# A hybrid encoder layer: zero products at the start, a DMA order, and three re-orderings around TensorE

## The chip, the cores and the metric

One core of a Trainium2 chip runs the whole layer in one launch. The metric is the device time of one execution in microseconds (us), as the median of several runs. TensorE (PE in the profile) multiplies and transposes, VectorE (DVE) and GpSimd (POOL) do elementwise work, ScalarE (ACT) evaluates functions and copies, SyncE (SP) issues most of the DMA transfers. PEld is TensorE's loading of weights.

## The reference

All in float32, one batch, 1024 tokens of width 1024. Three residual sub-layers:

```python
h = rms_norm(x, mix_pre_g)
proj = h @ w_in                        # u (512) | q, k, v (512 each) | 8 forget logits
y_ssm = s5_mixer(u, ...)               # diagonal state-space model, then GLU:
#   g = gelu(y);  out = g * sigmoid(g @ glu_w + glu_b)
y_fox = forgetting_attention(q, k, v, f_logit)        # 8 heads of 64, causal
y_mix = concat([rms_norm(y_ssm, ssm_out_g), rms_norm(y_fox, fox_out_g)])
x = x + rms_norm(y_mix @ w_out, mix_post_g)

h = rms_norm(x, xa_pre_g)              # cross-attention, 4 heads, 256 memory tokens
x = x + rms_norm(memory_cross_attention(h, rms_norm(mem, mem_g), ...), xa_post_g)

h = rms_norm(x, ffn_pre_g)             # SwiGLU, hidden width 2816
x = x + rms_norm((silu(h @ w_gate) * (h @ w_up)) @ w_down, ffn_post_g)
```

## The kernel before, in words

**Precision and products.** Each float32 operand is split into a rounded high part and a low part (`split`: a copy on ACT at L113 and a subtraction on DVE at L115 or L117). A product is then three matmuls, high by high, high by low and low by high (`mm3`, L122 to L124), accumulated in PSUM.

**Front (L896 to L926).** x comes transposed, in eight tiles of 128 rows by 1024 tokens; the u columns of `w_in` come as eight tiles of 128 by 512 (`u_load`). For each k one x tile and one weight tile are loaded and split, and `u_part` adds 24 matmuls into eight banks, four of pool `g` (`psg`) and two double ones of pool `s`. The first x tile is loaded and split in two halves (`x_fetch(xts, 0, 2)`, `x_split(..., 2)`), both ahead of the first weight tile in SP's queue.

**Projections and the state-space branch (L868 to L890).** The q, k and v projections run on TensorE while DVE computes the state-space scan. q and k go to DRAM (`qk_d`) and come back a head at a time. `ssm_out` (L629) then makes the branch's output: two slabs (`s_`), four groups of banks each (`b`), every group evacuated by a gelu on ACT (L639); then transposes and splits (L647, L649). The v tiles' evacuation is L310.

**Fox, GLU and fillers (L961 to L1002).** `fox` walks through 64 units, eight heads by eight blocks of 128 queries: `scores` (matmuls L733 and L734, DVE sum and minimum L740, exponential L742, normalisation L747), two units later `turn` (transposes L764, copied out of PSUM at L767 on DVE or L769 on ACT in turns), then `values` (L778). `prepare` loads the next head's q and k (L711, L712) and copies and splits them (L715, L716, L718); `behind()` orders those ACT copies after the last exponential that was issued, and before the first exponential there is nothing to order them after. Between fox units, `paced` steps the generator `fillers`: the rest of v, the GLU (`glu`: 12 matmuls, tanh L673, L674, L675, split, square L680, running sum L681 in `acc`, for four channel tiles by two token halves), the sums over channels for each token (`token_sums`, sixteen narrow matmuls L237, copied out at L238), `glu_stats` (the reciprocal root `r_s`), the memory's load, and `out_ssm`: row products of 12 matmuls into one bank of `g`, evacuated with the scale `r_s` on ACT (L836) and stored by SP (L839).

**The rest.** Output projection and first residual (L1018 to L1040), cross-attention, then the FFN with its products in a seven-multiplication scheme (L1260, L1518). At the end `take` and `quarter` process each quarter of the output: a DVE sum (L1462), its square on ACT with the row sum (L1453), the multiplication by the gain on POOL (L1459), and `finish`: `rsqrt_mean` (L137 to L145), the residual (L1497) and the store.

**Order.** A planner orders each engine's instructions ahead of time, by program order, priorities (`tc.high_priority`) and its own estimate of when each is ready; on the chip every engine then runs its list strictly in that order. `tc.issue_after(ins)` puts the instructions of a block that run on the engine of `ins` behind it in that list; it adds no wait. PSUM: four banks in pool `g`, used by nearly every product and transpose, and two double banks in pool `s`.

Of the kernel before, what the change touches and what calls it, by code (L numbers as in the profile page):

```python
# [9 lines left out]
F32 = mybir.dt.float32  # L10
# [7 lines left out]
P = 128  # L18
# [22 lines left out]
EVB = 13  # L41
OPB = 10


# [8 lines left out]
def layer(ctx: ExitStack, tc: tile.TileContext, a, out):  # L53
# [575 lines left out]
    def ssm_out():  # L629
        U, T, SS, mo = ssm_made  # L630
        for s_ in range(2):
            go = slab([P, 2, L, P], F32)
            with tc.high_priority(offset=boost):
                for b in range(4):
                    ps = g_ps([P, 4, NC])
                    for g in range(4):
                        pe.matmul(ps[:, g], U[s_][:, 4 * b + g], T[s_][:, 4 * b + g], start=True, stop=False)
                        pe.matmul(ps[:, g], SS[s_][:, 4 * b + g], mo[s_][:, 4 * b + g], start=False, stop=True)
                    act.activation(out=go[:, b // 2].rearrange("c j (g i) -> c g j i", i=16)[:, 4 * (b % 2):4 * (b % 2) + 4],  # L639
                                   in_=ps.rearrange("c g (j i) -> c g j i", i=16), func=AF.Gelu_apprx_tanh)  # L640
            yield
# [11 lines left out]
    def glu(ys):  # L653
# [9 lines left out]
        for ct in range(4):  # L663
            cs = slice(ct * P, (ct + 1) * P)
            hl = slab([P, 2, S])
            for h in range(2):
# [17 lines left out]
                yield  # L684
        token_sums(sv, acc)
        ys_stat.append(sv)

    def glu_stats():
        sv, = ys_stat
        tables("natural_log_exp_and_others")  # L690
        rsqrt_mean(r_s, sv, 512, 4 * EPS)


    def fox(yf):
# [3 lines left out]
        def prepare(h):  # L698
# [7 lines left out]
            for hf in range(2):  # L706
# [7 lines left out]
                with behind():  # L714
# [3 lines left out]
                    split(ka[:, 0, hs], ka[:, 1, hs], kd, lo_eng=eng)  # L718

        last = []  # L720

# [28 lines left out]
        def turn(h, t):  # L750
# [9 lines left out]
            for k0 in range(0, t + 1, 4):  # L760
# [4 lines left out]
                o = pt[:, k0:k0 + n, odd * P:(odd + 1) * P]  # L765
                if (t + k0 // 4) % 2:
                    dve.tensor_copy(o, tp[:, :n])  # L767
                else:
                    act.activation(out=o, in_=tp[:, :n], func=AF.Copy)  # L769
# [56 lines left out]
    def out_ssm(ys):  # L826
        for cc in range(4):
            wh, wl = load_w(a["w_out_s"][cc], 256)
            for j0 in range(0, NT, 2):
                o = t2t([P, 2, 256])  # L830
                for j in range(j0, j0 + 2):
                    ts = slice(j * P, (j + 1) * P)
                    ps = g_ps([P, 256])
                    for k in range(4):
                        mm3(ps, ys[k][:, 0, ts], ys[k][:, 1, ts], wh[:, k], wl[:, k], k == 0, k == 3)
                    act.activation(out=o[:, j - j0], in_=ps, func=AF.Copy, scale=r_s[:, j:j + 1])  # L836
                    if j == j0:
                        yield
# [16 lines left out]

    ys, yf, gl, ys_stat, r_mem, gate, ssm_made = [], [], [], [], [], [], []

# [38 lines left out]
    with tc.high_priority(offset=boost):  # L896
        xts = []
        x_fetch(xts, 0, 2)
        xs = [[slab([P, 2, S]) for _ in range(KT // 2)] for _ in range(2)]
        xH, xL = ([x[k // 2][:, k % 2] for k in range(KT)] for x in xs)  # L900
        acc_x = tt("d")
        banks = [g_ps([P, 512]) for _ in range(4)]
        banks += [b[:, h * 512:h * 512 + 512] for b in (s_ps([P, S]) for _ in range(2)) for h in range(2)]
        ws = [u_load(0)]
        x_split(xts, (xH, xL), 0, 2)
        u_part(banks, 0, ws[0], xH[0], xL[0])
# [55 lines left out]
    def fillers():  # L962
# [3 lines left out]
        rows = out_ssm(ys)  # L966
        glu_stats()
        for _ in mem_load(r_mem[0], mem):
# [479 lines left out]

    LO, HI = slice(0, 512), slice(512, 1024)

    def square(t, j, h, src):
# [3 lines left out]
    def quarter(t, j, hs):  # L1455

        c = acc[t][j][:, hs]
        square(t, j, 0 if hs is LO else 1, c)
        pool.tensor_tensor(out=c, in0=c, in1=g_fq[:, hs], op=ALU.mult)  # L1459

# [27 lines left out]
    def finish(t, j):  # L1488
# [7 lines left out]
        for hs in (LO, HI):  # L1496
            dve.scalar_tensor_tensor(out=x2[:, hs], in0=acc[t][j][:, hs], scalar=r, in1=x2[:, hs],  # L1497
                                     op0=ALU.mult, op1=ALU.add)
            if last:
# [90 lines left out]
```

## Time and profile before

| | us |
|---|---|
| median of 3 runs (lowest to highest) | 1423.64 (1420.83 to 1426.41) |
| the profiled execution | 1424.64 |
| its span, first to last instruction | 1422.9 |
| PE busy in the span | 1380.0 |
| DVE, ACT, POOL busy | 956.9, 653.7, 406.0 |
| mean granted TensorE clock | 0.989 of full |

A row of the trace gives the start and the duration in us, engine, line, operation and tiles, and in square brackets the idle time of the engine ahead of it with what ended it. A row of waits gives the waiting engine, tile and line, what it waited for, then the total in us, how often, and the longest.

### The profile page before, as it was taken

The numbers are of one execution on the slowest core, as the hardware profiler recorded it, in microseconds if no ns is written. First come the engines' busy times: TensorE is split into PE (matmuls) and PEld (weight loads), VectorE is DVE, ScalarE is ACT, GpSimd is POOL, SyncE is SP. The second block draws the span as 40 slices with busy tenths as digits, with TensorE's granted clock in tenths as the row PEclk, the third lists the DMA queues.
The fourth block names the chain that finished last, engine by engine and source line by source line (L and its number), as shares of the span: only waits on it lengthen the run. The fifth ranks groups of instructions, "written<-read, shape, count | busy, mean of one in ns | idle before, by whom it ended". The sixth has DMA issues, their size and how long they took to land.

```text
span 1422.9 us, 20364 instructions
## 1 busy us (share of the span) xinstructions
PE 1380.0 (97%) x7342; PEld 1165.1 (82%) x7342; DVE 956.9 (67%) x1703; ACT 653.7 (46%) x1293; POOL 406.0 (29%) x428
## 2 busy tenths in 40 slices
PE   7999989899999898999999999999999999999997
PEld 6889889789888686788888788888888888888886
DVE  8839945956566676645457677787777676565565
ACT  6372336666676555533434533333333334544351
POOL 0001000013333134002021367687666661000021
PEclk9999999999999998999999999999999999999999
DMA  6324653155643758324537355554444446965544
GB/s 208 95 77 134 172 177 105 58 166 178 202 146 106 183 184 249 116 74 135 176 115 258 123 185 185 179 172 164 151 156 155 170 148 228 346 210 192 178 163 163
DMA packets 110230, 234.22 MB, mean 165 GB/s; under 512 B 11816, under 2 KB 46632, under 8 KB 110000
## 3 DMA queue, kind: packets, MB, share of 16 engines
q1 hardware_dynamic: 94496, 179.91, 39.8%
q0 software_dynamic: 15632, 53.00, 10.4%
q8 instruction: 58, 0.95, 0.3%
q14 instruction: 44, 0.36, 0.1%
HBM read 166.81 MB, written 74.71 MB: 170 GB/s over the span
## 4 chain that ended last, share of the span: by engine, by line
PE 59%; DVE 1%; ACT 0%; issue 0%; DVEq 0%; ACTq 0%
PE x L1260 17%; PE g L1260 13%; PE x L1518 7%; PE g L1518 7%; PE x L123 2%; PE x L124 2%; PE x L122 2%; PE g L122 2%; PE g L123 2%; PE g L124 2%; PE g L1048 1%; PE g L1156 1%; DVE slab L115 0%; DVE whl L115 0%; DVE c L1039 0%; DVE rst L141 0%
## 5 line engine op out<-in xcount | busy, mean ns | idle before, releaser
L1260 PE MATMUL x<-slab,op 128*128 128x512 f32 x984 | 233.2, 389 | 0.5 <-DVE op L115 0.5
L1260 PEld LDWEIGHTS x<-slab,op 128*128 128x128 f32 x984 | 184.7, 188 | 39.2 <-DVE op L115 1.0
L1260 PE MATMUL g<-slab,op 128*128 128x512 f32 x744 | 178.7, 389 | 0.0
L115 DVE TENSOR_TENSOR slab<-slab 128x1024 fp32r<-128x1024 f32 (+2 forms) x92 | 110.5, 1207 | 84.6 <-ACT slab L113 82.6
L1260 PEld LDWEIGHTS g<-slab,op 128*128 128x128 f32 x744 | 139.7, 188 | 28.9
L122 PE MATMUL g<-slab,whl 128*128 128x512 f32 (+1 forms) x416 | 151.5, 364 | 1.7 <-ACT t L958 1.3
L124 PE MATMUL g<-slab,whl 128*128 128x512 f32 (+1 forms) x416 | 148.6, 358 | 0.0
L123 PE MATMUL g<-slab,whl 128*128 128x512 f32 (+1 forms) x416 | 148.5, 357 | 0.0
L113 ACT ACTIVATE slab<-slab 128x1024 fp32r<-128x1024 f32 (+2 forms) x92 | 95.0, 1037 | 105.0 <-DMA slab<-hs_d 75.0
L1518 PE MATMUL g<-slab 128*128 128x512 f32 x462 | 126.7, 389 | 0.0
L1518 PE MATMUL x<-slab 128*128 128x512 f32 x462 | 126.7, 389 | 0.0
L1518 PEld LDWEIGHTS x<-slab 128*128 128x128 f32 x462 | 86.7, 188 | 18.0
L1518 PEld LDWEIGHTS g<-slab 128*128 128x128 f32 x462 | 86.7, 188 | 18.0
L122 PE MATMUL g<-whl,slab 128*128 128x256 f32 (+2 forms) x288 | 88.5, 313 | 8.3 <-ACT whl L113 7.3
L115 DVE TENSOR_TENSOR whl<-raw,whl 128x1024 fp32r<-128x1024 f32 (+2 forms) x61 | 71.5, 1175 | 30.9 <-ACT whl L113 30.6
L115 DVE TENSOR_TENSOR op<-slab,op 128x512 fp32r<-128x512 f32 x80 | 83.4, 1053 | 11.5 <-ACT op L113 11.3
L1336 POOL TENSOR_TENSOR wt<-wt 128x256 f32<-128x256 f32 x88 | 83.5, 949 | 21.3 <-DMA wt<-in_w_down 17.7
L122 PEld LDWEIGHTS g<-slab,whl 128*128 128x128 f32 x416 | 78.6, 189 | 12.9 <-ACT t L958 1.5
L124 PEld LDWEIGHTS g<-slab,whl 128*128 128x128 f32 x416 | 78.4, 189 | 11.6 <-DVE whl L115 0.2
L123 PEld LDWEIGHTS g<-slab,whl 128*128 128x128 f32 x416 | 78.6, 189 | 10.6
L124 PE MATMUL g<-whl,slab 128*128 128x256 f32 (+2 forms) x288 | 86.9, 302 | 0.0
L123 PE MATMUL g<-whl,slab 128*128 128x256 f32 (+2 forms) x288 | 86.8, 301 | 0.0
(384 smaller groups left out, 2903.2 us busy)
## 6 DMA issues: line engine op xcount, KB each, us to landing
hs_d<-ev POOLq DMA_DIRECT2D x77, 256.0 KB, 2.6
slab<-hs_d SPq DMA_DIRECT2D x35, 512.0 KB
wt<-in_w_down SPq DMA_DIRECT2D x44, 256.0 KB
wt_d<-wt POOLq DMA_DIRECT2D x22, 512.0 KB, 4.8
slab<-in_w_gate SPq DMA_DIRECT2D x20, 512.0 KB
slab<-in_w_up SPq DMA_DIRECT2D x20, 512.0 KB
slab<-wt_d SPq DMA_DIRECT2D x20, 512.0 KB
wd_d<-in_w_down SPq DMA_DIRECT2D x33, 256.0 KB
```

The source lines that it names most:

```text
L113: first = act.activation(out=hi, in_=src, func=AF.Copy, scale=1.0 if mul is None else mul)
L115: (lo_eng or dve).tensor_tensor(out=lo, in0=src, in1=hi.bitcast(F32), op=ALU.subtract)
L122: pe.matmul(ps, lh, rh, start=first, stop=False)
L123: pe.matmul(ps, lh, rl, start=False, stop=False)
L124: pe.matmul(ps, ll, rh, start=False, stop=last)
L1048: pe.transpose(tp[:, k], src[:, (k0 + k) * P:(k0 + k + 1) * P], ident)
L1156: turned = pe.transpose(tp[:, k], h3[:, (4 * n + k) * P:(4 * n + k + 1) * P], ident)
L1260: pe.matmul(ps, x[:, k], y[:, k], start=first and k + n == 0, stop=k == 3 and n == 2, skip_group_check=not first)
L1336: pool.tensor_tensor(out=o, in0=x, in1=y, op=ALU.subtract)
L1518: pe.matmul(banks[n][j], xo[:, u, js], wo[:, v], start=ends[0] and k == 0, stop=ends[1] and k == 2, skip_group_check=onto is not None)
```

## The change

Five edits:

1. Front: DVE sets a 128 by 512 bf16 tile to zero, and TensorE multiplies it with itself 11 times into the first bank, whose content the first real product then overwrites. The first weight tile is loaded and split between the two halves of the first x tile, on SP's queue and in the program.
2. The list `last`, which `behind()` reads, now starts with the fourth gelu of `ssm_out`'s first slab. So the ACT copies of the first head's q and k stand behind that gelu.
3. `token_sums` moves from the end of `glu` into `glu_stats`, and `glu_stats` into `out_ssm`, behind the first two row products. The evacuation of both follows it. Each of the two products is a step of its own.
4. In `turn`, heads 0 and 1 copy all transposes on ACT (L769); the other heads take turns as before.
5. At the very end, one quarter's multiplication by the gain goes from POOL to DVE, into a tile of its own.

```diff
+WARM = 11
...
-                    act.activation(out=go[...], in_=ps..., func=AF.Gelu_apprx_tanh)
+                    g_ = act.activation(out=go[...], in_=ps..., func=AF.Gelu_apprx_tanh)
+                    if (s_, b) == (0, 3):
+                        last.append(g_)
...
+        ys_stat.append((sv, acc))
+
+    def glu_stats():
+        (sv, acc), = ys_stat
         token_sums(sv, acc)
-        ys_stat.append(sv)
-
-    def glu_stats():
-        sv, = ys_stat
         tables("natural_log_exp_and_others")
         rsqrt_mean(r_s, sv, 512, 4 * EPS)
...
-        last = []
...
-                if (t + k0 // 4) % 2:
+                if h > 1 and (t + k0 // 4) % 2:
                     dve.tensor_copy(o, tp[:, :n])
...
                 o = t2t([P, 2, 256])
+                made = []
                 for j in range(j0, j0 + 2):
                     ...
-                    act.activation(out=o[:, j - j0], in_=ps, func=AF.Copy, scale=r_s[:, j:j + 1])
+                    made.append((j, ps))
+                    if cc + j0 == 0:
+                        yield
+                        if j == 0:
+                            continue
+                        glu_stats()
+                    for jj, ps in made:
+                        act.activation(out=o[:, jj - j0], in_=ps, func=AF.Copy, scale=r_s[:, jj:jj + 1])
+                    made = []
                     if j == j0:
                         yield
...
-        x_fetch(xts, 0, 2)
+        x_fetch(xts, 0, 0)
...
+        def x_half(i):
+            cs = slice(i * 512, i * 512 + 512)
+            sp.dma_start(out=xts[0][1][:, cs], in_=a["xT"][0:P, cs])
+            return split(xH[0][:, cs], xL[0][:, cs], xts[0][1][:, cs], g_mix[:, 0:1])
...
+        still = tt("yt", [P, 512], BF16)
+        dve.memset(still, 0.0)
+        for _ in range(WARM):
+            pe.matmul(banks[0], still[:, 0:P], still, start=True, stop=True)
+        x_half(0)
         ws = [u_load(0)]
-        x_split(xts, (xH, xL), 0, 2)
+        x_half(1)
         u_part(banks, 0, ws[0], xH[0], xL[0])
...
         rows = out_ssm(ys)
-        glu_stats()
+        step(rows)
+        yield
         for _ in mem_load(r_mem[0], mem):
             step(rows)
             yield
...
         square(t, j, 0 if hs is LO else 1, c)
-        pool.tensor_tensor(out=c, in0=c, in1=g_fq[:, hs], op=ALU.mult)
+        if (t, j) == (1, 3) and hs is LO:
+            scaled.append(bp.tile([P, 512], F32, name="sq", tag="sq"))
+            dve.tensor_tensor(out=scaled[0], in0=c, in1=g_fq[:, hs], op=ALU.mult)
+        else:
+            pool.tensor_tensor(out=c, in0=c, in1=g_fq[:, hs], op=ALU.mult)
...
+            c = scaled[0] if last and hs is LO else acc[t][j][:, hs]
+            dve.scalar_tensor_tensor(out=x2[:, hs], in0=c, scalar=r, in1=x2[:, hs], op0=ALU.mult, op1=ALU.add)
```

More of the change, by code (lines that the diff above doesn't have):

```diff
@@ L638, in ssm_out @@
                         pe.matmul(ps[:, g], SS[s_][:, 4 * b + g], mo[s_][:, 4 * b + g], start=False, stop=True)
-                    act.activation(out=go[:, b // 2].rearrange("c j (g i) -> c g j i", i=16)[:, 4 * (b % 2):4 * (b % 2) + 4],
-                                   in_=ps.rearrange("c g (j i) -> c g j i", i=16), func=AF.Gelu_apprx_tanh)
+                    g_ = act.activation(out=go[:, b // 2].rearrange("c j (g i) -> c g j i", i=16)[:, 4 * (b % 2):4 * (b % 2) + 4],
+                                        in_=ps.rearrange("c g (j i) -> c g j i", i=16), func=AF.Gelu_apprx_tanh)
+                    if (s_, b) == (0, 3):
+                        last.append(g_)
             yield
@@ L854, in step @@
                 return
-    ys, yf, gl, ys_stat, r_mem, gate, ssm_made = [], [], [], [], [], [], []
+    ys, yf, gl, ys_stat, r_mem, gate, ssm_made, last = [], [], [], [], [], [], [], []
     def mem_stats():
@@ L1449, in layer @@
     LO, HI = slice(0, 512), slice(512, 1024)
+    scaled = []
     def square(t, j, h, src):
@@ L1496, in finish @@
         for hs in (LO, HI):
-            dve.scalar_tensor_tensor(out=x2[:, hs], in0=acc[t][j][:, hs], scalar=r, in1=x2[:, hs],
-                                     op0=ALU.mult, op1=ALU.add)
+            c = scaled[0] if last and hs is LO else acc[t][j][:, hs]
+            dve.scalar_tensor_tensor(out=x2[:, hs], in0=c, scalar=r, in1=x2[:, hs], op0=ALU.mult, op1=ALU.add)
             if last:
```

## The prediction

> **What bounds the kernel now.** I began with the busy times and the chain of waits on the page, then asked for TensorE's waits by stretch of the span, then for busy time and granted clock around each wait, and last for the instructions in order of time there.
>
> ```profile
> PE 1380.0 (97%) x7342; PEld 1165.1 (82%) x7342; DVE 956.9 (67%) x1703; ACT 653.7 (46%) x1293; POOL 406.0 (29%) x428
> ```
> ```profile
> PE g L122 <- ACT whl L113: 7.3, 1, 7.3
> ...
> PE g L237 <- DVE d L681: 5.4, 1, 5.4
> PE g L637 <- ACT t L310: 3.8, 1, 3.8
> PE g L764 <- ACT t L836: 2.0, 1, 2.0
> PE g L122 <- ACT slab L639: 0.4, 1, 0.4
> ...
> PE x L122 <- DVE a L1031: 4.6, 2, 4.1
> ```
>
> TensorE (PE) is busy for 97% of the span: whatever makes it idle, or slows it, moves the end, unless a later wait takes the time back. The wait rows give engine and line, the releaser, and microseconds, times and longest. Four of them touch the change: 7.3 us before the first product, then 3.8, 5.4 and 2.0 us between 150 and 300 us. The last row is a later stage, which I expect to keep its wait. The idle time isn't all that a wait costs. The next rows give, for one stretch each, its length, the busy time (and count) of PE, the weight loads, DVE, ACT and POOL, then the granted clock and the DMA's share and rate:
>
> ```profile
> 7.29:12.58 5.29, 5.29 (x13) 4.13 (x13) 4.46 (x7) 4.51 (x5) 0.00 (x0) 1.00 1.00 372
> 12.58:30.00 17.42, 17.42 (x78) 14.45 (x77) 17.10 (x30) 13.73 (x18) 0.00 (x0) 1.00 0.58 195
> 265.00:272.90 7.90, 2.50 (x14) 1.84 (x12) 6.93 (x14) 5.73 (x12) 1.78 (x1) 0.94 0.00 0
> 272.90:278.65 5.75, 5.70 (x27) 5.70 (x28) 4.92 (x11) 4.37 (x9) 1.28 (x1) 0.50 0.18 63
> ...
> 286.00:288.40 2.40, 0.39 (x4) 0.10 (x2) 2.10 (x3) 2.40 (x6) 1.16 (x1) 1.00 0.34 118
> 288.40:292.20 3.80, 3.80 (x21) 3.80 (x22) 2.93 (x5) 2.37 (x5) 1.85 (x2) 0.59 0.79 238
> 196.30:200.30 4.00, 0.18 (x3) 0.03 (x1) 0.41 (x1) 1.05 (x3) 0.00 (x0) 1.00 0.79 175
> 200.30:204.00 3.70, 3.65 (x16) 3.46 (x16) 0.28 (x1) 1.56 (x2) 0.55 (x1) 0.54 0.12 40
> ```
>
> After each of the three inner waits the granted clock is about half: 0.54, 0.50, 0.59. Work lost there is busy time times one minus clock. So wait one costs 4.00 - 0.18 = 3.82 idle plus 3.65 x 0.46 = 1.68, and 0.36 for the row on L639, 5.9 us in all; wait two 7.90 - 2.50 = 5.40 plus 5.70 x 0.50 = 2.85, 8.25 us; wait three 2.01 plus 3.80 x 0.41 = 1.56, 3.6 us. At the start the clock reads 1.00, but 13 products take 5.29 us (0.407 each) where later 78 take 17.42 (0.223 each): the same half pace, before the record of the clock begins. At full pace the 13 would take 2.90, so 2.39 us are lost there.
>
> **The front.**
>
> ```profile
> 0.81 0.06 DVE L92 MEMSET ones<- 128x1 f32 x1 [0.81 <-PEq L1582]
> ...
> 1.20 0.89 SPq L205 DMA_DIRECT2D slab<-in_xT  x2
> ...
> 2.13 0.43 SPq L259 DMA_DIRECT2D raw<-in_w_u  x1
> ...
> 3.85 1.54 ACT L113 ACTIVATE slab<-slab,gains 128x512 fp32r<-128x512 f32 x2 [1.83 <-DMA slab<-in_xT]
> ...
> 6.61 0.63 ACT L113 ACTIVATE whl<-raw 128x512 fp32r<-128x512 f32 x1 [0.27 <-DMA raw<-in_w_u]
> ...
> 10.02 0.63 PE L123 MATMUL g<-whl,slab 128*128 128x512 f32 x1
> ...
> 11.59 0.69 DVE L115 TENSOR_TENSOR whl<-raw,whl 128x512 fp32r<-128x512 f32 x1
> ...
> 12.58 0.40 PE L123 MATMUL g<-whl,slab 128*128 128x512 f32 x1
> ```
> ```profile
> L568 DVE MEMSET c<- x1: 485/485/485, 48.8 to 48.8; 128x512 f32 x1
> ```
>
> The first product waits for the weights: they are issued behind both halves of x (2.13) and reach ScalarE (ACT) at 6.61, while the second half was ready for it within 3.85 + 1.54 = 5.39. With the weights in the second half's place on SP's queue (no transfer more or less; the second half is one place later) they should be split by about 5.4. The new memset can begin at 0.81 and costs at most the 0.49 of the larger one at L568, so the zero products can start at 1.3. Their price isn't in the trace; the nearest rows are slow products of 512 columns, six from 10.02 to 12.58, 0.427 each: 11 x 0.427 = 4.7, to 6.0 us. The real products stand behind them in order, so the start moves from 7.29 to 6.0: 1.29 us. From the first product to full pace took 5.29 us; from 1.3 that is 6.6, so 0.6 us of real products are still slow and cost 0.3 of the 2.39. Next to be late is the second weight tile: its low part is ready at 11.59 + 0.69 = 12.28, where the 24 products of the first now end near 6.0 + 24 x 0.223 + 0.3 = 11.7; I take 0.3 for that. Front: 1.29 + 2.39 - 0.3 - 0.3 = 3.1 us. Lower end 1.0 (the pace stays slow, the two waits stay), upper 4.3 (5.4 as start, no wait, full pace).
>
> The Trainium skill, "TensorE: Matmul & The Clock Gate", Part 1, says that the gate opens after a busy window of about 3.4 us that runs free of the kernel's start. By that, full pace comes 3.4 to 6.8 us after 1.3, and the 0.3 would lie between 0 and 1.05; the trace's 5.29 agrees.
>
> **The first head's copies behind a gelu.**
>
> ```profile
> 191.35 1.00 SPq L712 DMA_DIRECT2D d<-qk_d  x1
> ...
> 199.23 0.63 ACT L715 ACTIVATE a<-d 128x512 fp32r<-128x512 f32 x1 [8.91 <-DMA d<-qk_d]
> ...
> 226.88 0.65 ACT L113 ACTIVATE slab<-e 128x512 fp32r<-128x512 f32 x1
> ```
>
> ACT stands for 8.91 us in head 0's query copy L715, whose data were issued until 192.35 and landed at 199.2. Behind it stand the evacuation L310 and the gelus of `ssm_out`, whose products fill the four PSUM banks of pool g. `issue_after` orders only on ACT: head 0's four copies (L715 and L113, twice) now stand behind the fourth gelu, and the gelus run as their products end. The copies' user, `scores` of head 0, isn't made later: its key copies ran only at 226.88 anyway. Behind a waiting L715 are now the splits of the gelu's transposes and one L310, for some 2 us; TensorE has three freed banks by then. I take 5.2 of the 5.9. Ends: 2.0 (the wait moves behind the gelu and holds L310 as before, at the price of wait three with its slow clock) and 5.9.
>
> **GLU sums behind two row products; ScalarE copies.**
>
> ```profile
> L767 DVE COPY slab<-g 128x512 f32<-128x512 f32 x3 | 2.1, 690 | 0.9 <-PE g L764 0.9
> ```
> ```profile
> 240.00:260.00 20.00, 20.00 (x107) 16.65 (x106) 19.68 (x44) 15.34 (x31) 0.00 (x0) 1.00 0.26 85
> ```
> ```profile
> 271.55 0.75 DVE L117 SCALAR_TENSOR_TENSOR slab<-t,gains,slab 128x512 fp32r<-128x512 f32 x1 [0.79 <-ACT slab L113]
> ...
> 272.95 1.87 PE L237 MATMUL g<-ones,d 128*128 128x1 f32 x8 [5.37 <-DVE d L681]
> ...
> 276.02 0.68 DVE L681 TENSOR_TENSOR d<-d,t 128x512 f32<-128x512 f32 x1
> ...
> 279.75 0.95 PE L237 MATMUL g<-ones,d 128*128 128x1 f32 x8
> ...
> 283.54 0.16 DVE L238 COPY sv_s<-g 128x8 f32<-128x8 f32 x1
> ...
> 287.89 1.19 ACT L836 ACTIVATE t<-g,r_s 128x256 f32<-128x256 f32 x3
> ...
> 288.40 0.66 PE L764 MATMUL g<-ident,c 128*128 128x128 f32 x4 [2.01 <-ACT t L836]
> ```
>
> Wait two: the sums L237 need `acc` from VectorE (DVE), which is late. In the new order the row products stand first. They need the last `ys`, whose first half is done at 271.55 + 0.75 = 272.3, hardly before the sums' 272.95. Only 9 of the 12 matmuls of each product (k below 3) don't need it: at half of 0.223, for 256 columns instead of 512, two products cover 2.0 us. So without a faster DVE the reorder alone saves about 2 us. The copies are the other half: DVE is full from 240 to 260 us (19.68 of 20), and six copies a head go to ACT (widths 256, 512, 128, 512, 384, 512). At 690 ns for 512 columns a head's 2304 are 3.1 us off DVE, and about as much on ACT (15.34 of 20). I let `ys` come 2.5 us earlier: idle 5.40 - 2.0 - 2.5 = 0.9.
>
> Wait three: the row products hold banks until r_s; its sums were completed at 279.75 + 0.95 only, copied at 283.54, and L836 freed the first bank after 287.89. Now all sixteen sums stand behind two row products, whose evacuations, ACT's table load and the first store on SP's queue (behind it there: the loads of a later head) stand behind them. The sums can't be before 276.02 + 0.68 less the 2.5, about 274; then some 2 us of r_s chain. Two row products and the sums hold three of the four banks until then, so I leave 2.0 us of idle as in that row, and 1.95 us of slow clock, between wait three's 1.56 and wait two's 2.85. Saved: 8.25 + 3.6 - 0.9 - 2.0 - 1.95 = 7.0 us. Ends: 2.0 (cover alone) and 11.8 (all of both).
>
> The Trainium skill, "TensorE: Matmul & The Clock Gate", section "Why this matters for your kernels", says that idle gaps up to about 3 us keep the clock. By that the 1.95 would go, and the total be 17.2 instead of 15.2; but here 2.01 us of idle were followed by a clock of 0.59, so I keep it.
>
> A copy on ACT can also hold a bank longer, behind exponentials: I take 0.7 us against the change, ends -0.5 and 4.0 (twice wait three's 2.0).
>
> **The tail.**
>
> ```profile
> 1415.68 1.26 POOL L1459 TENSOR_TENSOR acc<-acc,g_fq 128x512 f32<-128x512 f32 x1 [6.18 <-ACT sq L1453]
> ...
> 1416.20 0.76 DVE L141 SCALAR_TENSOR_TENSOR rst<-rsy,rsv 128x1 f32<-128x1 f32 x1 [0.35 <-ACT rsy L138]
> ...
> 1416.99 0.16 DVE L145 SCALAR_TENSOR_TENSOR r<-rst,rsy 128x1 f32<-128x1 f32 x1
> ```
>
> L141 ends (1416.96) with POOL's multiply (1416.94), though L145, as small, takes 0.16. With the multiply on DVE (about 0.7, while ACT squares and DVE has nothing to do) L141 should take 0.16: 0.6 us saved, ends 0 and 0.7.
>
> **Sum.** 3.1 + 5.2 + 7.0 - 0.7 + 0.6 = 15.2 us. The profiled execution took 1424.64; the median of the runs, 1423.64, is 1.0 lower. 1423.6 - 15.2 gives 1408.4.
>
> **Rivals.** (a) Wait two only moves: DVE frees nothing that the GLU chain uses, since ACT receives what DVE loses and the chain passes through both. Then parts three and four give 2.0 less 0.7 and the sum is 3.1 + 5.2 + 1.3 + 0.6 = 10.2: 1413. For it: the half of `ys` at 272.3; against it: DVE at 19.68 of 20. (b) Zero products don't raise the clock: the sum loses 2.1, 1410.5; no row shows products of zeros. (c) Little arrives: ends of the front and of wait one together with (a), 1.0 + 2.0 + 1.3 + 0.6 = 4.9: 1418.7, no change. (d) Slower: ACT becomes the pace of heads 0 and 1. Twelve copies move to it; if each holds TensorE as L836 held it, 2.0 idle plus 1.56 of clock, the price is 42 us. It decides from five such holds on (18 us against the 15.9 of the rest); for the 0.5% it takes seven. ACT at 15.34 of 20 speaks against more than one or two. (e) Everything goes: 4.3 + 5.9 + 11.8 + 0.6 + 0.5 = 23.1: 1400.5.
>
> **How the numbers follow.** Forecast 0.50 with (b) inside it at 0.10 more, (a) 0.18, (c) 0.11, (d) 0.05, (e) 0.06. About 0.5% (7 us) is what a measurement of this kernel can tell from no change. Faster: 0.50 + 0.10 + 0.18 + 0.06 = 0.84; same 0.11; slower 0.05. The range runs from 1401 (next to all of (e)) to 1418 (just short of (c)), leaving out about 0.18.
>
> **What would show it.** Right: first real product near 6.0 with 0.22 us spacing soon after; no L637 wait on L310 and a clock of 1.00 past 200; L715 behind four L639; no wait of L237 over 1 us; L141 at 0.16. Wrong: products still 0.42 apart after the zeros; TensorE waits on L769 adding up to several us before 300; a wait at the first row product as long as wait two; or the gain found by 300 us given back before 600, where the copies' stage and L1031 have waits of their own.

## The result, and the profile after

| | before | changed |
|---|---|---|
| median, us | 1423.66 | 1418.86 |
| lowest to highest changed run, us | | 1414.65 to 1422.82 |
| ratio (95% interval) | | 0.9967 (0.9958 to 0.9976) |
| the profiled execution, us | 1424.64 | 1421.36 |
| its span, us | 1422.9 | 1419.6 |

4.8 us were gained where 15.2 were forecast; the time lies 0.9 us above the upper end of the forecast's range. One execution of e4 (2313 us) and one of e17 (2796 us) were slow ones and are left out of their medians. With the line `WARM` every line number of the changed kernel is one or more higher: L122 is L123, L237 is L238, L740 is L741, L778 is L779, L946 is L967, L958 is L979.

The page's busy times of the changed kernel, and TensorE's waits over the whole span (microseconds, times, longest):

```profile
PE 1384.8 (98%) x7353; PEld 1163.4 (82%) x7353; DVE 946.7 (67%) x1693; ACT 659.7 (46%) x1305; POOL 405.5 (29%) x427
```
```profile
PE g L779 <- ACT t L979: 4.0, 1, 4.0
...
PE s L734 <- DVE nlr L741: 3.0, 1, 3.0
...
PE s L452 <- ACT d L176: 1.3, 1, 1.3
...
PE g L638 <- ACT t L311: 0.6, 1, 0.6
```

TensorE is idle for 1419.6 - 1384.8 = 34.8 us of the span (42.9 before), though the span is only 3.3 us shorter: the 4.7 us of zero products count as busy. The waits of 7.3, 5.4, 3.8 and 2.0 us are gone, and others stand in the list: one of 4.0 us that no step of the prediction has, one of 3.0 for the scores' reduction L741. What a stretch costs TensorE is its idle time plus busy time times one minus clock. The windows of before and then of the changed kernel (length, PE, PEld, DVE, ACT, POOL busy, granted clock, DMA):

```profile
180.00:260.00 80.00, 75.72 (x523) 69.47 (x522) 43.57 (x85) 42.53 (x79) 4.86 (x9) 0.98 0.44 139
260.00:280.00 20.00, 14.55 (x80) 12.90 (x79) 17.30 (x37) 14.58 (x29) 3.06 (x2) 0.83 0.08 27
280.00:300.00 20.00, 17.71 (x129) 15.47 (x129) 15.68 (x40) 13.49 (x30) 3.02 (x2) 0.91 0.60 185
360.00:380.00 20.00, 19.68 (x166) 17.18 (x166) 11.68 (x24) 11.94 (x25) 6.30 (x6) 1.00 0.81 243
400.00:420.00 20.00, 20.00 (x160) 17.95 (x160) 12.63 (x32) 14.02 (x32) 8.34 (x8) 1.00 0.44 136
```
```profile
180.00:260.00 80.00, 78.87 (x553) 71.53 (x552) 45.95 (x93) 47.98 (x93) 4.87 (x9) 1.00 0.41 133
260.00:280.00 20.00, 14.96 (x85) 12.44 (x83) 19.87 (x41) 16.22 (x34) 6.09 (x4) 0.80 0.26 80
280.00:300.00 20.00, 18.95 (x152) 16.33 (x151) 10.17 (x25) 13.47 (x31) 0.61 (x1) 0.95 0.52 165
360.00:380.00 20.00, 15.97 (x114) 12.47 (x114) 6.73 (x20) 8.17 (x21) 2.98 (x4) 0.83 0.53 173
400.00:420.00 20.00, 17.97 (x130) 15.21 (x129) 12.07 (x25) 12.74 (x28) 9.65 (x7) 0.91 0.36 112
```

| lost in | before | changed | gained |
|---|---|---|---|
| 180 to 260 us (the gelu edit) | 5.8 | 1.1 | 4.7 |
| 260 to 300 us (sums and copies) | 11.8 | 10.0 | 1.8 |
| 360 to 380 us | 0.3 | 6.7 | -6.4 |
| 400 to 420 us | 0 | 3.7 | -3.7 |

The gelu edit did what was forecast: the first head's query copies (L718, at 199.01 us) stand behind four gelus (L640, from 197.08). The sums and copies gained 1.8 us at their place, and about 10 us were lost in stretches that the prediction didn't cost. To follow such gains I use the lead below: how much earlier than in the kernel before TensorE has done the same number of product columns. It is worked out from the start times of all matmuls of two traces, and the times given with it are those of the kernel before. Fourteen traces with the same front had leads of 3.2 to 4.3 us at 58 us, so one profile doesn't settle less than 1 us.

### The profile page after: what moved, and what is told of

It is laid out like the page before. It is cut to its first block, busy times and chain, and to the rows that moved or that the text cites. A ratio compares the mean times of both kernels' runs of the same rounds, so it can differ in the third digit from the quotient of the medians.

```text
span 1419.6 us, 20383 instructions
## 1 busy us (share of the span) xinstructions
PE 1384.8 (98%) x7353; PEld 1163.4 (82%) x7353; DVE 946.7 (67%) x1693; ACT 659.7 (46%) x1305; POOL 405.5 (29%) x427
## 4 chain that ended last, share of the span: by engine, by line
PE 59%; DVE 1%; ACT 0%; issue 0%; DVEq 0%; ACTq 0%
PE x L1282 17%; PE g L1282 13%; PE x L1545 7%; PE g L1545 7%; PE x L124 2%; PE x L125 2%; PE g L123 2%; PE x L123 2%; PE g L125 2%; PE g L124 2%; PE g L1070 1%; PE g L1178 1%; DVE c L1061 0%; DVE whl L116 0%; ACT yt L1055 0%; DVE rst L142 0%
## 5 line engine op out<-in xcount | busy, mean ns | idle before, releaser
L116 DVE TENSOR_TENSOR slab<-slab 128x1024 fp32r<-128x1024 f32 (+2 forms) x92 | 110.0, 1207 | 85.0 <-ACT slab L114 83.8
L123 PE MATMUL g<-slab,whl 128*128 128x512 f32 (+1 forms) x416 | 151.8, 365 | 0.6 <-ACT whl L114 0.4
L116 DVE TENSOR_TENSOR whl<-raw,whl 128x1024 fp32r<-128x1024 f32 (+2 forms) x61 | 71.2, 1170 | 36.3 <-ACT whl L114 36.1
L116 DVE TENSOR_TENSOR op<-slab,op 128x512 fp32r<-128x512 f32 x80 | 84.0, 1061 | 11.6 <-ACT op L114 11.3
L123 PE MATMUL g<-whl,slab 128*128 128x256 f32 (+2 forms) x288 | 86.6, 309 | 4.3 <-ACT t L845 2.9
L123 PEld LDWEIGHTS g<-slab,whl 128*128 128x128 f32 x416 | 78.6, 189 | 11.9 <-ACT whl L114 0.6
L125 PEld LDWEIGHTS g<-slab,whl 128*128 128x128 f32 x416 | 78.4, 189 | 11.8 <-DVE whl L116 0.2
L114 ACT ACTIVATE op<-slab 128x512 fp32r<-128x512 f32 x80 | 50.0, 628 | 81.2 <-PE x L1282 38.3
L124 PE MATMUL g<-whl,slab 128*128 128x256 f32 (+2 forms) x288 | 86.2, 299 | 0.0
```

The costliest lines, as they stand in the source:

```text
L114: first = act.activation(out=hi, in_=src, func=AF.Copy, scale=1.0 if mul is None else mul)
L116: (lo_eng or dve).tensor_tensor(out=lo, in0=src, in1=hi.bitcast(F32), op=ALU.subtract)
L123: pe.matmul(ps, lh, rh, start=first, stop=False)
L124: pe.matmul(ps, lh, rl, start=False, stop=False)
L125: pe.matmul(ps, ll, rh, start=False, stop=last)
```

## Experiments: each edit by itself

Here each run is the kernel before with the part of the change's diff that is named.

**The front alone** (e1): edit 1.

```diff
-        x_fetch(xts, 0, 2)
+        x_fetch(xts, 0, 0)
...
+            pe.matmul(banks[0], still[:, 0:P], still, start=True, stop=True)
+        x_half(0)
         ws = [u_load(0)]
+        x_half(1)
```

> Edit 1 alone (zero products, weights between the halves of x). Theory A: TensorE gains 3.7 us in the front, but VectorE is full there with the state-space constants and finishes r_x at about 71 us whatever TensorE does, so the lead over the kernel before falls to about 1.8 us by 90 us and the time is about 2 us shorter. Rival B: the lead was lost by another of the edits; alone it keeps 3.7 us past 90 us and the time is 3 to 4 us shorter.

1421.88 us, ratio 0.9991 (0.9977 to 1.0004): not told from no change. The lead is 3.4 us until 78 us, 2.3 at 88 us, 2.3 at the end, much as theory A has it.

**The front without its zeros** (e12), in e1:

```diff
-WARM = 11
+WARM = 0
```

> The front alone with the x loaded and split by halves around the weights, but without the eleven products of zeros. Theory A (the zeros raise the clock): the first real products start at 5.5 us or a little earlier and run at half clock for about 3 to 4 us as in the kernel before; the lead of 3.4 us at 18 us falls to 0.5 to 1.5 us; time 1422 to 1424 us, 0.5 to 1.5 us over the run e1. Rival B (the order of the loads and splits is what brought the lead, the zeros only fill the wait): the lead at 18 us stays 3 us or more and the time is that of e1, 1421.5 to 1422.

1423.11 us, ratio 0.9998 (0.9985 to 1.0010). The time doesn't part it from e1, the trace does. Its windows from the first product on:

```profile
5.69:10.04 4.35, 4.35 (x11) 3.44 (x11) 2.60 (x7) 3.54 (x4) 0.00 (x0) 1.00 1.01 384
10.04:20.00 9.96, 9.96 (x45) 8.26 (x44) 9.86 (x18) 8.08 (x12) 0.00 (x0) 1.00 0.86 281
```

Eleven products take 0.395 us each, then 45 take 0.221. The lead from 16 to 70 us is 2.1 us in place of e1's 3.4: the order of the loads brought 2.1, the zeros 1.3, in these two traces. Measured against the 3.2 to 4.3 us of the fourteen, the zeros bring 1.1 to 2.2. Neither theory had that share for the order.

**The gelu edit alone** (e2): edit 2.

```diff
+                    if (s_, b) == (0, 3):
+                        last.append(g_)
```

> Edit 2 alone (the first head's copies behind the fourth gelu). Theory A: the wait of 3.8 us and its slow clock go, a lead of about 5 us by 215 us; what is left of it at the end says how much the stages up to 500 us give back: at least 3 us shorter. Rival B: the row of VectorE's work at 260 to 290 us doesn't begin earlier when TensorE does, and the lead is gone by 290 us: less than 1 us shorter.

1418.12 us, ratio 0.9962 (0.9949 to 0.9975): 5.1 us, as much as the whole change. Theory A is borne out: the lead is 5.3 us at 215 us, and it is kept.

**The sums alone** (e3): edit 3.

```diff
-        token_sums(sv, acc)
-        ys_stat.append(sv)
+        ys_stat.append((sv, acc))
...
+                    if cc + j0 == 0:
+                        yield
+                        if j == 0:
+                            continue
+                        glu_stats()
```

> Edit 3 alone (sums of the GLU behind two row products). Theory A: VectorE is the bound from 260 to 290 us; the wait of 5.4 us at the sums becomes a wait at the row products or at the scores, TensorE's idle time from 260 to 300 us is 5 us or more, and the time changes by less than 2 us. Rival B: as in the prediction, 2 us from the cover and most of wait three: 4 to 6 us shorter.

1427.59 us, ratio 1.0030 (1.0017 to 1.0042), slower by 4.3. TensorE's waits from 180 to 430 us:

```profile
PE g L237 <- DVE d L681: 4.9, 1, 4.9
...
PE g L778 <- ACT t L967: 3.0, 1, 3.0
PE g L764 <- DVE sv_s L238: 2.2, 1, 2.2
```

The sums wait as before, as theory A says, but the time is longer, which neither theory had. The wait of the products with v (L778) for the copy of a memory tile (L967) is new, and the runs without edit 3 (e1, e2, e4) don't have it.

**The copies alone** (e4): edit 4.

```diff
-                if (t + k0 // 4) % 2:
+                if h > 1 and (t + k0 // 4) % 2:
```

> Edit 4 alone (heads 0 and 1 copy on ScalarE). Theory A: VectorE has 6 us less to do from 235 to 290 us, the wait at the sums is 1 to 3 us shorter and the time 1 to 3 us. Rival B: ScalarE holds the banks longer; TensorE waits for L769 several times before 300 us and the time is longer.

1428.1 us, ratio 1.0036 (1.0024 to 1.0048), slower by 4.9. In the same stretch:

```profile
PE g L764 <- ACT d L788: 4.2, 1, 4.2
...
PE g L237 <- DVE d L681: 3.6, 1, 3.6
```

The sums wait 3.6 us in place of 5.4, and the transposes behind them 4.2 for ScalarE in place of 2.0. So theory A has the sums' wait right, and rival B that the time is longer, though the wait isn't for L769.

**Sums and copies together** (e5): the last two diffs.

> Edits 3 (GLU sums behind two row products) and 4 (ScalarE copies for heads 0 and 1) on the kernel before, without front, gelu edit and tail. Alone, edit 3 cost 4.3 us and edit 4 cost 5.1 us. Theory A: both wait for the same thing, VectorE's list at 262 to 292 us (edit 3 alone: the sums wait 4.9 us for VectorE's running total; edit 4 alone: the transposes wait 4.2 us for ScalarE), so each needs the other: together 1423 to 1426 us, the wait of the sums under 1.5 us. Rival B: the two costs are separate and add up: 1431 to 1434 us. Whichever it is, the matmuls' waits at 300 to 420 us seen with edit 3 alone (3.0, 2.1, 1.1 us) should stay, since the copies are not done there.

1426.45 us, ratio 1.0022 (1.0008 to 1.0036). They don't add up: together they cost 3.2 us, less than either alone. The wait of the sums is 0.3 us, as theory A has it, that of L778 3.8; the time is just over its range.

**The change without edits 3 and 4** (e10): the changed kernel with the last two diffs undone.

> The changed kernel without edits 3 and 4: front, gelu edit and tail alone, nothing else. It parts the 10.1 us of the run e8 into what the early scale of x brought and what leaving edits 3 and 4 out brought. Theory A (edits 3 and 4 together cost time inside the changed kernel, about the 3.2 us that they cost together on the kernel before): 1415 to 1417 us. Rival B: most of e8's gain is the early scale of x, and edits 3 and 4 are about even: 1418 to 1419.5 us. Rival C: all of it is edits 3 and 4: 1413 to 1414 us.

1413.84 us, ratio 0.9933 (0.9918 to 0.9948), against 0.9967 for the whole change. So edits 3 and 4 cost some 5 us inside it, more than the 3.2 outside: rival C.

## Experiments: the loss at 360 to 380 us

SyncE's queue around the load of the second half of v (L796, 1 MB), before and then changed:

```profile
359.64 0.38 SPq L158 DMA_DIRECT2D raw<-in_w_out_s  x1
...
365.65 0.33 SPq L158 DMA_DIRECT2D raw<-in_w_out_s  x1
...
368.85 0.50 SPq L796 DMA_DIRECT2D slab<-v_d  x1
...
370.57 1.44 SPq L158 DMA_DIRECT2D raw<-in_w_out_s  x1
```
```profile
352.96 0.33 SPq L159 DMA_DIRECT2D raw<-in_w_out_s  x1
...
356.16 0.38 SPq L797 DMA_DIRECT2D slab<-v_d  x1
...
358.10 2.00 SPq L159 DMA_DIRECT2D raw<-in_w_out_s  x1
```

The v load belongs to a unit of the heads (head 3, unit 5), the weight loads to the fillers. Edit 3 adds a step to the fillers, the one with the sums and no product, so the fillers behind it come one step later against the units: two row weight loads stood ahead of the v load, now one does. ScalarE's list there, TensorE's, and two windows:

```profile
367.44 1.06 ACT L114 ACTIVATE whl<-raw 128x1024 fp32r<-128x1024 f32 x1 [5.74 <-DMA raw<-in_w_out_s]
368.41 0.37 ACT L979 ACTIVATE t<-g 128x256 f32<-128x256 f32 x1
```
```profile
368.83 4.96 PE L779 MATMUL g<-slab 128*64 128x256 f32 x24 [4.03 <-ACT t L979]
```
```profile
366.00:369.00 3.00, 0.17 (x2) 0.18 (x4) 0.47 (x1) 1.55 (x3) 0.00 (x0) 0.74 0.39 156
368.83:374.00 5.17, 5.17 (x26) 2.90 (x27) 1.09 (x2) 1.45 (x5) 0.61 (x1) 0.50 0.62 178
```

The split of that weight, wanted only by later fillers, waits 5.74 us on ScalarE; behind it stands the copy L979, which frees a bank; TensorE idles 4.03 us, and then runs 5.17 us at a clock of 0.50, which costs 2.6 more.

**The v load three units later** (e7), in the changed kernel:

```diff
-                if (h, t) == (3, 5):
+                if (h, t) == (4, 0):
                     load_v(1)
```

> The changed kernel with the load of the second half of v begun three units later (head 4 unit 0 in place of head 3 unit 5), so that it isn't issued just ahead of the output weights. Theory A: the 4.0 us for which TensorE waits at 368.8 us comes from ScalarE's weight split, which waits 5.74 us for a weight load that lies behind that load of v. Then the wait falls under 1 us, the lead at 378 us rises from 3.0 to 7 or more, and the time is 1413.5 to 1416 us. Rival B: the weight load is late because its buffer comes free late, the v load has no part in it: wait and time stay, 1418 to 1420 us. Rival C: the load of v is late for head 4's values, which wait instead: no gain, a new wait of the products with v at 380 to 420 us.

1419.02 us, ratio 0.9966 (0.9950 to 0.9983), the wait 3.9 us. It tested nothing: the planner put the load back just ahead of the same weight load (358.23 and 359.34 us), so neither rival is borne out.

**The v load much later** (e9), so that it stands behind the last row weight:

```diff
-                if (h, t) == (3, 5):
+                if (h, t) == (4, 6):
```

> The changed kernel with the load of the second half of v begun at head 4 unit 6, so that on SyncE's list it now stands behind the last of the ssm output weights and not ahead of them (in the run e7 it had kept its place). Theory A: the 4.0 us wait of TensorE at 368.8 us and the half clock behind it come from a weight load that lies behind this 1 MB load of v. Then the wait goes, the clock of 360 to 380 rises from 0.83 to 1.00, the lead at 378 us is 7 or more in place of 3.0, and if it is kept the time is 1413 to 1416 us. Rival B: the weight load's buffer comes free late and v has no part in it: the wait stays above 3 us, 1418 to 1420 us. Rival C: the wait goes but the lead is lost again before 600 us, because the units there have waits of their own: 1416.5 to 1419 us.

1411.72 us, ratio 0.9915 (0.9898 to 0.9931), under theory A's range. The same split, and the window:

```profile
362.04 1.06 ACT L114 ACTIVATE whl<-raw 128x1024 fp32r<-128x1024 f32 x1 [1.21 <-DMA raw<-in_w_out_s]
```
```profile
360.00:380.00 20.00, 20.00 (x171) 17.01 (x170) 10.17 (x27) 12.48 (x29) 7.29 (x7) 1.00 0.53 172
```

The split waits 1.21 us in place of 5.74, TensorE not at all, and the clock is 1.00. The place of one load was worth 7.1 us, more than the whole change had gained; the window's 6.7 accounts for nearly all of it.

**Edits 3 and 4 with the v load out of the way** (e13, e14, e15): e9 without both, without 4, without 3.

> Front, gelu edit and tail, with the v load at head 4 unit 6 as in e9; without edits 3 and 4. Compared with e9 (1411.7 us) it gives what edits 3 and 4 bring together once the v load is out of their way. Theory A (they save 1 to 3 us at 265 to 292 us, not the 7.0 predicted, since the wait and the half clock only move to the scores' reduction): 1412.5 to 1414 us. Rival B (the v load had also cost e10 its lead at 360 to 380 us, so most of e9's gain is the v load alone): 1410.5 to 1412 us, edits 3 and 4 worth nothing. Rival C (they bring what was predicted): 1416 us or more, which would mean that the v load costs nothing here.

> The changed kernel with the v load at head 4 unit 6, without edit 4 (copies again by turns on VectorE and ScalarE for heads 0 and 1): edit 3 alone among the two. Theory A (both edits relieve the same list, VectorE's at 262 to 292 us, and each needs the other: without edit 4 the token sums wait some 5 us for VectorE's running total, as in e3): 1413.5 to 1416 us, that wait 3.5 us or more. Rival B (edit 4 has no part in it): 1411 to 1412.5 us.

> The changed kernel with the v load at head 4 unit 6, without edit 3 (the sums again before the row products): edit 4 alone among the two. Theory A: the wait of the sums for VectorE's total is 3 to 4 us in place of 5.4, but the transposes behind wait 3 to 4 us for ScalarE as in e4: 1413 to 1416 us. Rival B (edit 3 has no part in it): 1411 to 1412.5 us.

| v load at (4, 6) | without edit 4 | with edit 4 |
|---|---|---|
| without edit 3 | 1415.48, 0.9945 (0.9934 to 0.9957) | 1415.72, 0.9944 (0.9932 to 0.9956) |
| with edit 3 | 1413.08, 0.9929 (0.9917 to 0.9941) | 1411.72, 0.9915 (0.9898 to 0.9931) |

Together they bring 3.8 us. Edit 4 alone brings nothing, edit 3 alone 2.4; whether the copies add anything behind edit 3 (1.4 us) lies within the intervals. Only e15 came out in its theory A's range: e13 lies between the ranges of A and C, e14 a little under A's, though the sums' wait there is 4.9 us as A says. Without edits 3 and 4 the v load's place does nothing that can be told (e13 0.9945, e10 0.9933): its collision belongs to edit 3.

## Experiments: the stall at 265 to 280 us

VectorE's list in the changed kernel, and TensorE's wait:

```profile
265.54 1.78 DVE L677 TENSOR_TENSOR t<-slab 128x512 f32<-128x512 f32 x1
267.25 1.08 DVE L967 TENSOR_TENSOR raw<-raw,t 128x256 f32<-128x256 f32 x3
268.25 0.68 DVE L678 SCALAR_TENSOR_TENSOR t<-t,t 128x512 f32<-128x512 f32 x1
268.86 1.75 DVE L967 TENSOR_TENSOR raw<-raw,t 128x256 f32<-128x256 f32 x5
270.53 0.94 DVE L741 CUSTOM_DVE_ANT_0 c<-s,b 128x768 f32<-128x768 f32 x1
...
273.26 0.67 DVE L684 TENSOR_TENSOR d<-d,t 128x512 f32<-128x512 f32 x1
```
```profile
271.54 0.55 PE L734 MATMUL s<-slab,a 128*128 128x512 f32 x1 [3.01 <-DVE nlr L741]
```

In the kernel before, the memory operands' multiplies stood behind the GLU's last running total, L681 at 276.02:

```profile
276.62 2.76 DVE L946 TENSOR_TENSOR raw<-raw,t 128x256 f32<-128x256 f32 x8
```

In the changed kernel that total (L684) stands at 273.26, six microseconds behind the first multiplies. In the traces with edit 3 and the memory's load in its place (e3, e5, e7, e9, e14, e16, e18) the multiplies stand ahead of that total, in those without edit 3 behind it, but for e4. The likely reason, which wasn't tested, is that the sums are no longer ahead of them in the program. With that they also stand before the scores' reduction, for which TensorE then waits.

**The memory's operands later** (e6), in the changed kernel:

```diff
         step(rows)
         yield
+        for _ in range(8):
+            step(rows)
+            yield
         for _ in mem_load(r_mem[0], mem):
```

> The changed kernel with the memory operands' load, multiply and split begun eight fillers later (eight more steps of the row products stand ahead of them). Theory A: at 265 to 277 us VectorE is the bound (19.87 us busy of 260 to 280), and the memory's eight multiplies and eight splits of 128x256 stand ahead of the scores' reduction, for which TensorE idles 3.01 us, after which it runs at half clock to about 276 us. Without them there that wait falls under 1 us, the clock of 260 to 280 rises from 0.80 to over 0.93, and the lead over the kernel before at 288 us rises from 8.5 to 12 or 13 us; if it is kept, the time is 1414 to 1415.5 us. Rival B: the same operations collide with the units eight fillers later, the lead is lost by 330 us: 1418 to 1420 us. Rival C: the wait belongs to the sums' chain and stays whatever the memory does: no change in the trace at 266 to 276 us.

1414.05 us, ratio 0.9928 (0.9912 to 0.9944). The time came out as theory A has it, the trace did not. At 288 us the lead is 10.0 us (12 to 13 expected, and the clock of 260 to 280 us is 0.74); at 318 us it is 10.9, and at 328 us 4.4, since TensorE now waits there:

```profile
PE s L734 <- DVE nlr L744: 3.6, 1, 3.6
PE g L238 <- DVE d L684: 2.1, 2, 1.9
```

The stall moves with the memory's operations, as rival B says. The time was gained behind 360 us: the weight loads stand elsewhere again, and L779's wait is 1.6 us.

**Without the multiplies** (e17), in e9:

```diff
-                dve.tensor_tensor(out=m[:, kk], in0=m[:, kk], in1=rb, op=ALU.mult)
```

> The kernel of e9 with the eight multiplies of the memory's operands by their row scales left out (the memory is split unscaled, so this part of the computation is missing); everything else as in e9. In the changed kernel and in e9 they take 2.8 us of VectorE ahead of the scores' reduction for which TensorE idles 3.0 us at 268 to 271 us and after which it runs at half clock for some 10 us (5 us lost). Theory A: they are what remains of the stall: the wait falls under 1 us, the clock of 260 to 280 rises from 0.76 to 0.95 or more, the lead at 298 us rises by 4 to 7 us, and if it is kept the time is 1405 to 1408 us. Rival B: VectorE's list there is longer than these operations, another wait of 2 us or more takes the place (the GLU's running total, the splits), and the half clock stays: 1410 to 1412 us.

1409.07 us, ratio 0.9903 (0.9882 to 0.9924), e9 0.9915: between the two theories' ranges, and not told from e9. The trace bears out rival B, though its largest single wait is 1.7 us. Windows:

```profile
260.00:280.00 20.00, 14.34 (x85) 11.54 (x83) 18.25 (x36) 17.47 (x36) 5.49 (x4) 0.84 0.32 98
280.00:300.00 20.00, 19.63 (x153) 17.16 (x153) 7.37 (x21) 12.07 (x28) 0.61 (x1) 0.90 0.45 147
```

TensorE loses 5.66 + 14.34 x 0.16 + 0.37 + 19.63 x 0.10 = 10.3 us in the two windows, as much as with them (9.8 in e9). The one wait of 3.0 us is replaced by nine of 0.2 to 1.7 us, for VectorE and for ScalarE by turns. VectorE is busy for 18.25 of 20 us, ScalarE for 17.47: both lists are full there, and no single group of operations is the stall.

## Experiments: the front's lost lead, and versions with all mends

VectorE and ScalarE in the changed kernel, where the lead falls from 3.2 to 1.7 us:

```profile
68.56 2.28 DVE L444 TENSOR_TENSOR slab<-slab 128x2048 f32<-128x2048 f32 x1
...
70.95 0.17 DVE L146 SCALAR_TENSOR_TENSOR r_x<-rst,rsy 128x8 f32<-128x8 f32 x1
```
```profile
71.15 3.31 ACT L282 ACTIVATE slab<-slab,r_x 128x256 f32<-128x256 f32 x8 [7.55 <-DVE r_x L146]
74.37 1.16 ACT L114 ACTIVATE whl<-raw 128x1024 fp32r<-128x1024 f32 x2
75.44 1.06 ACT L176 ACTIVATE d<-s 128x512 f32<-128x512 f32 x2
```

TensorE came 3.2 us earlier to x's sums, but VectorE, whose list has no gap from 57.9 to 71 us, gives their scale r_x only at 71.1, where the kernel before had it at 71.3. ScalarE then scales, splits a weight and copies the row (L176), and TensorE waits 1.3 us.

**The scale of x ahead, without edits 3 and 4** (e8), in e10:

```diff
-        r_x, row = x_stats(acc_x)
+        with tc.high_priority(offset=boost):
+            r_x, row = x_stats(acc_x)
```

> The changed kernel without edits 3 and 4 (front, gelu edit and tail only), and with the sums, scale and row of x scheduled ahead of other work of their region. Theory A: the front's lead is 3.4 to 3.8 us and falls to 2 us at 80 us because VectorE's 128x2048 operations stand ahead of x's scale, so that ScalarE copies x's row late; put ahead, the lead at 88 us stays 3 us or more; and front (1.4), gelu edit (5.1) and tail (0.6) as measured alone or read add up: with another 1 to 2 us from the scale of x, 1414 to 1415.5 us, faster than the changed kernel. Rival B: the lead falls at 80 us all the same (ScalarE's weight split stands there): 1416 to 1416.5. Rival C: the gains do not add, since the two stalls at 265 and 286 us take a part back: 1417 us or more.

1413.15 us, ratio 0.9919 (0.9903 to 0.9935). In its trace:

```profile
66.07 0.16 DVE L146 SCALAR_TENSOR_TENSOR r_x<-rst,rsy 128x8 f32<-128x8 f32 x1
```

The lead at 88 us is 4.6 us (2.2 in e10): the cause is shown. But the median is only 0.7 us under e10's, within the intervals. The time is under theory A's range; what that theory had wrong is the price of edits 3 and 4, not this.

**The same on e9** (e18), the same diff:

> The kernel of e9 with the scale of x ahead, as in e8, and nothing else. The lead at 88 us is 4.4 to 4.6 us in place of 3.1. Theory A: the shift passes on, 1410 to 1411.5 us, the same as e16, whose order of the memory's splits then did nothing. Rival B: the shift is lost in the units behind: 1411.5 to 1413 us, and e16's order of the splits was worth about 1 us.

1411.90 us, ratio 0.9913 (0.9897 to 0.9930): the time of e9. The lead at 88 us is 3.7 (3.1 in e9), at the end 11.2 (11.5): what was kept at 80 us is lost behind, and rival B holds for that part. The 3.7 is less than the 4.4 to 4.6 expected.

**All mended** (e11: e18 with e6's eight steps; e16: e18 with this):

```diff
+                with tc.issue_after(last[-1].ins):
                     dve.tensor_tensor(out=m[:, kk], in0=m[:, kk], in1=rb, op=ALU.mult)
                     split(mh[:, k + kk], ml[:, k + kk], m[:, kk], g_mem[:, k + kk:k + kk + 1])
```

> All five edits, with the scale of x ahead (as in e8), the memory's operands eight fillers later (as in e6) and the v load at head 4 unit 6. If what the three mends bring adds up (2.5 to 3 us for x, 4.8 us of e6, of which 0.7 us was the front's, and the lost lead at 322 and 365 us): 1410 to 1413 us, the best of all. Rival: the fillers' places against the heads' units decide more than the mends: anywhere from 1413 to 1417 us, with new waits at 320 to 420 us.

> All five edits, the v load at head 4 unit 6, the scale of x ahead as in e8, and the memory operands' multiplies and splits ordered behind the last exponential, which moves only six of the eight splits behind the scores' reductions that they stood ahead of; the eight multiplies keep their place. Theory A: the lead at 88 us rises from 3.1 to 4.5 us and the wait behind the scores' reduction stays near 3 us, since it is the multiplies (2.8 us) that stand ahead of it, but less is lost behind: 1409.5 to 1411 us, the best of all. Rival: the shift of 1.4 us is lost again in the units, as when all was mended together in e11: 1411.5 to 1414 us.

e11: 1416.19 us, ratio 0.9946 (0.9930 to 0.9961), slower than e9: its lead falls from 14.2 to 6.7 at 318 to 328 us, where the memory's operations now stand, as the rival has it. e16: 1411.21 us, ratio 0.9909 (0.9894 to 0.9923), the fastest version that computes everything, and not told from e9, which differs from the changed kernel in one line; it lies between the two ranges.

## Why the prediction was wrong

| step | forecast | found |
|---|---|---|
| front | 3.1 | lead of 3.7 at 20 us, 1.8 left at 98; alone 1.4 in time, within the noise |
| gelu edit | 5.2 | 4.7 in its window; alone 5.1 |
| sums and copies | 7.0 - 0.7 | 1.8 in their window; -5.0 in time (the change against e10) |
| tail | 0.6 | 0.5 by rows |

**Front: right at its place, in its sum.** Zeros from 1.19 us, real products from 5.50 (6.0 forecast), and full pace, 0.23 us apart, soon behind the first of them:

```profile
1.19 4.71 PE L923 MATMUL g<-yt 128*128 128x512 bf16 x11 [1.19 <-DVE epsc L96]
...
5.50 1.32 PE L123 MATMUL g<-whl,slab 128*128 128x512 f32 x4
...
6.66 0.39 PE L124 MATMUL g<-whl,slab 128*128 128x512 f32 x1
6.89 0.39 PE L125 MATMUL g<-whl,slab 128*128 128x512 f32 x1
```

Eleven products of zeros take 4.71 us, as costed, and the first four real ones 1.16 to the next. Rival (b) is refuted: they raise the clock. The shares are not those of the forecast, which put 1.3 us on the earlier start and 2.1 on the pace: without the zeros (e12) the order of the loads gave 2.1 by itself. Unstated was that a lead must pass every later place where another engine is the pace: 1.5 us of it ended at r_x.

**Gelu edit: right.** L638's wait is 0.6 us, and 180 to 260 us run at 1.00.

**Sums and copies: the step that failed** is "Saved: 8.25 + 3.6 - 0.9 - 2.0 - 1.95 = 7.0 us". It left 4.85 us of the 11.8 lost there; 10.0 were lost. The sums' own wait did go, to 0.5 us, and r_s no longer holds banks for long. The input that failed is "I let `ys` come 2.5 us earlier": the last running total came at 273.26 in place of 276.02, while TensorE was 6.5 us ahead at 260 us, so that measured against TensorE it came 3.7 us later. I counted on a VectorE relieved of copies, and didn't ask what else stands in its list and in what order. The memory's multiplies were in this stretch before too, behind the total; now they stand ahead of it and of the scores' reduction, and VectorE is busy for 19.87 of 20 us (17.30 before). e17 shows that leaving them out doesn't help either: there VectorE (18.25) and ScalarE (17.47), to which edit 4 gives the copies, hold TensorE by turns. At its place the outcome is that of rival (a), "Wait two only moves": it put 1.3 us on both parts, and the window shows 1.8. Its reason isn't borne out, since the copies alone did shorten the sums' wait, from 5.4 to 3.6 us (e4, e15).

**The step that was missing** is the filler's shift. By rival (a) the time would have been 1413; e9 has 1411.7. What lies between the two and 1418.9 is the weight load that edit 3 pushes behind v. The prediction asked what stands behind the first store on SP's queue, but not what becomes of the loads of the fillers behind the step that moved; it put this at nothing. It cost 7.1 us. The prediction's last sign of being wrong, the gain found by 300 us given back before 600, is what happened, though not at the places it named. That the time agrees with rival (c), 1418.7, is chance: front and gelu edit brought what the forecast gave them, not (c)'s lower ends. The forecast took 7 us as what can be told from no change; here 4.8 us could be, since the interval ends at 0.9976.

**Tail: right.** L142 takes 0.22 us (0.76 before), and from the last sum to the issue of the last two stores 3.27 us in place of 3.81.

**The clock behind a wait.** The forecast kept 1.95 us of slow clock against the Trainium skill, "TensorE: Matmul & The Clock Gate", section "Why this matters for your kernels", which lets gaps of up to about 3 us pass. Here 3.01 us of idle were followed by a clock of 0.53 for 4.46 us and 0.50 for 4.00 more:

```profile
271.54:276.00 4.46, 3.82 (x13) 2.89 (x13) 4.46 (x11) 4.44 (x12) 0.51 (x1) 0.53 0.17 32
276.00:280.00 4.00, 3.50 (x16) 3.38 (x16) 3.96 (x8) 2.06 (x5) 2.91 (x2) 0.50 0.65 231
```

This gap lies at that limit and doesn't speak against it; the 2.01 us before a clock of 0.59, in the kernel before, does. But 2 us is no threshold either. Over the 20 traces, after the first 20 us, all 44 gaps of TensorE of 2.63 us or more had a granted clock of 0.5 between 1 us before and 5 us after their end; of the 29 gaps of 2.0 to 2.6 us 15 had one and 14 none (e9 has 2.44 us at 408 us, in a window at 1.00).

**Still open:** what makes the 3.8 us that edits 3 and 4 bring once v is out of the way. In the windows of 260 to 300 us TensorE loses 11.6 us in e13, 12.4 with edit 3 alone (e14), 10.1 with edit 4 alone (e15) and 9.8 with both (e9): at their place the copies gain and the sums don't, in time it is the other way round. The rest comes later. Between 418 and 598 us e9's lead grows from 8.2 to 12.0, while e13's is 6.5 at both ends; 3.4 us of it come at 550 to 560 us, where TensorE waits for the first residual, a wait that the prediction expected to stay: 4.5 us in e13 (L1043), 4.1 in the kernel before (L1031) and 1.1 in e9 (L1053). But e10, which has neither edit, has 1.1 us too, so this wait isn't shown to belong to the edits, and each of these is one execution. The loss at 400 to 420 us, which e9 still has (2.4 us for L845), is of the kind of the loss at 360: L845 stands closely behind ScalarE's copy L718, which waits 3.20 us there for the load of the next head's q and k (2.77 in the changed kernel). What makes that load late wasn't tested.

## What to carry to other kernels

Before costing a wait as removed, list what else stands in the same stretch on the engines that feed it: with VectorE at 17 and ScalarE at 15 of 20 us, the wait went to the next in line. A step moved in a chain of fillers shifts every load issued behind it; look in the DMA queue for a large transfer among them, and in the in-order list of the engine that waits for the load for what stands behind. Time each edit alone before summing: here one edit by itself had all of the gain, and two cost time until one load was moved.

## What the hardware showed that was not expected

Products of zeros raise the clock as others do, and when they do varies from one execution to the next. In the fourteen traces with zeros the pace doubled 2.9 to 5.9 us after the first zero product (4.8 in the changed kernel; in e9 and e17 2.9, so that the last zeros ran at full pace already), in the six without them 3.5 to 5.7 us after the first real one (5.3 in the kernel before, 4.35 in e12). So one trace doesn't give the price of a slow start to better than some 1 us, and three of the traces (e9, e13, e17) lie under the 3.4 us from which the prediction counted.

Elementwise operations of VectorE can stretch beside GpSimd's: L677 takes 0.68 us at 255.28 and 1.78 at 265.54, where GpSimd runs a split (L116, 265.39 to 266.78).
